# Gathering an expert's rows in quarters and turning them on VectorE instead of TensorE, in a one-core transformer layer on Trainium2

## The chip, the cores and the metric

The kernel runs on one NeuronCore of one Trainium2 chip. A core has five engines with instruction queues of their own, each run in order: TensorE (PE in the rows, PEld for its weight loads), VectorE (DVE), ScalarE (ACT), GpSimd (POOL) and SyncE (SP), and 16 DMA engines that they share. SP issues most of the plain transfers, GpSimd all the indirect ones. The metric is the device time of one execution in microseconds.

## What is computed

The reference is one layer of a diffusion backbone in float32: a token mixer, then a mixture of 64 small experts over 1,024 tokens of width 1,024. The change is in the second half. Each token picks 8 experts, and each expert has two products of 1,024 by 256 (gate and up) and one of 256 by 1,024 (down):

```python
_, idx = lax.top_k(s + b_router, TOP_K)                 # 8 of 64 experts per token
wts = s_sel / jnp.sum(s_sel, axis=-1, keepdims=True) * ROUTE_SCALE
...
xb = hpad[rows]                                          # the rows of one block of one expert
y = (jax.nn.silu(xb @ we_gate[e]) * (xb @ we_up[e])) @ we_down[e]
return acc.at[rows].add(y * rw[:, None].astype(y.dtype)), None
...
shared = (jax.nn.silu(hf @ ws_gate) * (hf @ ws_up)) @ ws_down
return (acc[:nt] + shared).reshape(B, T, D)
```

So 8,192 rows are gathered, sent through their expert's products, weighted and added back; a shared expert runs over all 1,024 tokens besides.

## The kernel before

A first part (mixer and router, about 570 us) writes the normalised rows to DRAM as `hx`, 1,024 rows of 1,024 features followed by the token's 64 expert weights (`XW` = 1,088 columns), and builds on chip, for each of 98 blocks, a column of row numbers: `tok` for the gather, `dst` for the scatter.

Then `moe` runs the experts' stage. `BLOCKS` lists 102 blocks: four of the shared expert (tiles of 128 tokens; three at the head, one at the end) and 98 of the routed experts, 48 of 128 rows, 23 of 80 to 120, 16 of 64 and 11 of 32. The last four token tiles of the shared expert are done in `final`. `pipeline.run` goes through the blocks in software-pipelined order. In the turn of block i it issues gate and up products of block i (`stage_gu`), the down product and the scatter of block i-1 (`stage_dn`), the turning of the hidden vector of block i (`stage_ht`), then `stage_x` of block i+2 and `gather` of block i+3. The order in each engine's queue is made by a scheduler from this program; a gather waits until its buffer, one of three (`xg`), has been read.

- `gather` (L1429 on) is one indirect DMA on GpSimd's queue (L1439): up to 128 rows of 1,088 values, one per partition. Rows beyond the list are skipped by the bounds check.
- `stage_x` (L1444 on) turns the rows, since TensorE wants features on partitions: eight transposes of 128 by 128 through TensorE into PSUM (`px`, L1461; L1454 for blocks of 64 and 32 rows). For the larger blocks the turned rows are then split into a rounded high part and a low remainder: ACT casts (`xH`, L50) and VectorE subtracts (`xL`, L51), each in two halves of 512 columns. Small blocks are copied by ACT only (`xR`).
- `row_weight` (L1347) picks the row's weight out of the 64 gathered with it, one VectorE instruction and an accumulator read.
- The weights of an expert, three parts of 1 MB, are loaded by SP (L1426) into a pool of buffers (`u`) and split in the same way: cast on ACT, subtraction on VectorE (`u<-u,u`, both inputs in SBUF, 128 x 1,024, L50 and L51). Blocks of more than 64 rows use three matmuls per product (L436 to L438, the split parts), smaller blocks one.
- The scatter (L1559) is an indirect DMA on GpSimd that adds the block's result into one of two accumulators (`acc`) in DRAM.

[...]

## Time and profile before

| | us |
|---|---|
| median of three runs (1,494.69 to 1,501.90) | 1,495.82 |
| the profiled execution | 1,497.91 |
| its span in the trace | 1,496.1 |
| TensorE busy in the span | 1,426.1 (95%) |
| VectorE | 1,133.3 (76%) |
| ScalarE | 753.7 (50%) |
| GpSimd | 477.9 (32%) |
| mean load of the 16 DMA engines, 573 to 1,433 us | 0.95 |

The experts' stage lies between the first gather at 573.8 us and the last accumulating write at 1,433 us; what follows is `final`, some 60 us. Busy time is the time in which an engine executes something; an engine that waits in its queue is idle. A row of the timeline gives the start, the length, the engine, the line, the operation, output and inputs, and in brackets the idle time before it and what ended that.

### The profile page before, as it was taken

The page shows a single profiled execution, that of the slowest core. Times are in us where ns is not written, and L with a number is a line of the kernel's source. Part 1 is how long each engine was busy: PE and PEld are TensorE (multiplying, and loading weights), DVE is VectorE, ACT ScalarE, POOL GpSimd, SP SyncE. Part 2 cuts the span into 40 slices and gives each one's busy share as a digit, 9 for nine tenths or more (in the row PEclk, how much of TensorE's full clock was granted, in tenths as well). Part 3 has the DMA queues.
Part 4 walks back from the last instruction along what each step waited for, and adds up shares of the span by engine and source line. Part 5 has one row for each costly group of instructions (what it writes and reads, how often), then busy time and mean ns, then how long its engine had stood idle before and what let it go on. Part 6 is the DMA issues. An engine that isn't in the chain of part 4 may idle for free. (4 is left out here: it accounts for less than half of the span.)

```text
span 1496.1 us, 22962 instructions
## 1 busy us (share of the span) xinstructions
PE 1426.1 (95%) x8211; PEld 1088.5 (73%) x8211; DVE 1133.3 (76%) x1942; ACT 753.7 (50%) x1241; POOL 477.9 (32%) x306
## 2 busy tenths in 40 slices
PE   6999999989999989999999999999999999999975
PEld 4688997765567755876788888888777777777764
DVE  5899979767867886744678788888777877777636
ACT  4421011245433344644566666776676767666621
POOL 1245001112213422233333333333334344455324
PEclk9999999999999999999999999999999999999998
DMA  8421051018653567997999999999999999999975
GB/s 314 176 71 43 1 189 40 19 48 287 221 187 115 193 240 275 357 294 246 306 288 327 331 322 319 333 343 339 316 342 299 321 342 310 315 352 318 337 251 209
DMA packets 94385, 371.64 MB, mean 248 GB/s; under 512 B 18269, under 2 KB 26789, under 8 KB 67770
## 3 DMA queue, kind: packets, MB, share of 16 engines
q1 hardware_dynamic: 65946, 298.48, 53.3%
q0 software_dynamic: 26032, 70.19, 19.2%
q10 hardware_dynamic: 2288, 1.45, 0.4%
q8 instruction: 66, 1.08, 0.3%
q14 instruction: 53, 0.43, 0.1%
HBM read 322.38 MB, written 62.19 MB: 257 GB/s over the span
## 5 line engine op out<-in xcount | busy, mean ns | idle before, releaser
L51 DVE TENSOR_TENSOR u<-u,u 128x1024 fp32r<-128x1024 f32 x354 | 422.0, 1220 | 124.7 <-ACT u L50 94.8
L50 ACT CAST u<-u 128x1024 fp32r<-128x1024 f32 x354 | 361.3, 1052 | 108.5 <-PE pgu L438 41.6
L1559 POOL DMA_INDIRECT acc<-yb,dst x98 | 194.4, 1983 | 351.7 <-ACT hTH L50 118.3
L436 PE MATMUL pgu<-u,xH 128*128 128x512 f32 x608 | 245.8, 404 | 0.4
L437 PE MATMUL pgu<-u,xH 128*128 128x512 f32 x608 | 238.8, 393 | 0.0
L438 PE MATMUL pgu<-u,xL 128*128 128x512 f32 x608 | 238.1, 392 | 0.0
L1439 POOL DMA_INDIRECT xg<-hxd,tok x98 | 123.6, 1261 | 194.1 <-DVE rwj L1347 68.6
L431 DVE SCALAR_TENSOR_TENSOR X<-X,cw 128x912 f32<-128x912 f32 (+14 forms) x120 | 152.0, 1291 | 1.1
L436 PEld LDWEIGHTS pgu<-u,xH 128*128 128x128 f32 x608 | 114.5, 188 | 25.5 <-ACT u L50 2.6
L438 PEld LDWEIGHTS pgu<-u,xL 128*128 128x128 f32 x608 | 114.3, 188 | 24.6
L437 PEld LDWEIGHTS pgu<-u,xH 128*128 128x128 f32 x608 | 114.5, 188 | 21.5
L436 PE MATMUL py<-u,hTH 128*128 128x512 f32 x304 | 122.1, 402 | 0.5 <-ACT hTH L50 0.5
L437 PE MATMUL py<-u,hTH 128*128 128x512 f32 x304 | 119.8, 394 | 0.0
L438 PE MATMUL py<-u,hTL 128*128 128x512 f32 x304 | 118.6, 395 | 0.0
L436 PE MATMUL pf<-hH,wfH 128*128 128x512 f32 x256 | 103.6, 408 | 0.0
L437 PE MATMUL pf<-hL,wfH 128*128 128x512 f32 x256 | 102.7, 401 | 0.7 <-DVE hL L226 0.6
L51 DVE TENSOR_TENSOR xL<-px,xH 128x512 fp32r<-128x512 f32 x152 | 97.5, 681 | 7.7 <-ACT xH L50 7.3
L438 PE MATMUL pf<-hH,wfL 128*128 128x512 f32 x256 | 102.3, 400 | 0.0
L50 ACT CAST xH<-px 128x512 fp32r<-128x512 f32 x152 | 83.9, 592 | 13.7 <-PE pgu L437 7.8
L1551 DVE COPY yb<-py 128x512 f32<-128x512 f32 x75 | 51.5, 687 | 46.3 <-PE py L438 45.8
L51 POOL TENSOR_TENSOR wfL<-wfr,wfH 128x1024 fp32r<-128x1024 f32 x14 | 48.0, 3428 | 118.2 <-ACT wfH L50 104.2
L1461 PE MATMUL px<-ident,xg 128*128 128x128 f32 x600 | 83.8, 274 | 1.1 <-DVE nl L1244 1.1
(431 smaller groups left out, 2515.6 us busy)
## 6 DMA issues: line engine op xcount, KB each, us to landing
u<-in_we_dram SPq DMA_DIRECT2D x192, 1024.0 KB
wa<-in_wa_dram SPq DMA_DIRECT2D x64, 256.0 KB
wa<-in_wa_dram SPq DMA_DIRECT2D x8, 1024.0 KB
wfr<-in_wf_dram SPq DMA_DIRECT2D x16, 512.0 KB
v<-acc SPq DMA_DIRECT2D x16, 512.0 KB
acc<-zero SPq DMA_DIRECT2D x13, 512.0 KB
u<-in_ws_dram SPq DMA_DIRECT2D x6, 1024.0 KB
X<-in_xT_dram SPq DMA_DIRECT2D x8, 512.0 KB
```

The source lines that it names most:

```text
L50: self.nc.scalar.copy(H, src)
L51: return (eng or self.nc.vector).tensor_tensor(L, src, H.bitcast(F32), op=OP.subtract).ins
L431: nc.vector.scalar_tensor_tensor(y[:, :, a:b], u[:, :, a + o:b + o], cw[:, i:i + 1], y[:, :, a:b], op0=OP.mult, op1=OP.add)
L436: mm(out, lH, rH, start=start, stop=False, skip_group_check=free)
L437: mm(out, lH, rL, start=False, stop=False, skip_group_check=free)
L438: mm(out, lL, rH, start=False, stop=stop, skip_group_check=free)
L1439: nc.gpsimd.indirect_dma_start(out=x[:n], out_offset=None, in_=self.hx, in_offset=bass.IndirectOffsetOnAxis(ap=self.tok[:n, c:c + 1], axis=0),
L1461: nc.tensor.transpose(pt[:, k], x[:, (4 * q + k) * 128:(4 * q + k) * 128 + 128], self.ident)
L1551: nc.vector.tensor_copy(y[:, 512:], py)
L1559: nc.gpsimd.indirect_dma_start(out=self.acc[b % NA].rearrange("r (n d) -> (r n) d", n=n), in_=y[:rows], in_offset=None, out_offset=bass.In ...
```

## The change

The gathered rows are no longer turned on TensorE.

- The routed rows come in groups of 32 and quarters of the width. One indirect DMA brings 32 rows: each row of `hx` is read as four rows of 256, and partition 32q + a gets quarter q of row a. A block needs one such DMA per 32 rows, rounded up. Their row numbers are made once, in `route`: the list is bounded from above, copied to the four partition quarters by 16 small matmuls and scaled (`tokq`).
- VectorE then turns all 32 by 32 blocks of the tile in one instruction, from SBUF to SBUF (`STREAM_TRANSPOSE`). Partition 32q + a' of the result holds feature 256q + 32f + a' for f = 0 to 7, and the host lays out the gate and up weights in this order, so that the products run as before.
- The split of the turned rows is one cast and one subtraction of 1,024 columns out of SBUF. Small blocks need no copy. The tile between (`xT`) has one buffer.
- A row's weight is no longer gathered with the row. It is fetched as a single element by an indirect DMA of its own per block (`row_weights`, list `widx`, from the new tensor `hw`) into one of eight columns.
- The shared expert's tiles are loaded by four DMAs each instead of one.

```diff
+        tf = rp.tile([128, NB], F32, name="tf", bufs=1)
+        nc.vector.tensor_scalar(tf, self.tok, 2.0 * NX - 1, None, op0=OP.min)
+        pq = bank("pT4", [128, 4, NB])
+        for g in range(4):
+            for q in range(4):
+                mm(pq[32 * q:32 * q + 32, g], self.ident[:, 32 * g:32 * g + 32], tf, start=True, stop=True,
+                   skip_group_check=True)
+        nc.vector.tensor_scalar(self.tokq, pq, 4.0, self.part[:, 1:2], op0=OP.mult, op1=OP.add)
+        nc.vector.scalar_tensor_tensor(self.widx, tf, float(NE), self.eb, op0=OP.mult, op1=OP.add)
...
-        self.xg = [gp.tile([128, XW], F32, name=f"xg{i}") for i in range(3)]
+        self.xg = [gp.tile([128, 4, 256], F32, name=f"xg{i}") for i in range(3)]
...
-        n = HB if rows == HQ else rows
-        nc.gpsimd.indirect_dma_start(out=x[:n], out_offset=None, in_=self.hx,
-                                     in_offset=bass.IndirectOffsetOnAxis(ap=self.tok[:n, c:c + 1], axis=0),
-                                     bounds_check=NX - 1, oob_is_err=False)
+        for g in range(-(-rows // 32)):
+            nc.gpsimd.indirect_dma_start(out=x[:, g], out_offset=None, in_=self.hx.rearrange("t (q d) -> (t q) d", q=4),
+                                         in_offset=bass.IndirectOffsetOnAxis(ap=self.tokq[:, g, c:c + 1], axis=0),
+                                         bounds_check=4 * NX - 1, oob_is_err=False)
...
+    def load_tile(self, x, j):
+        for q in range(4):
+            self.nc.sync.dma_start(x[32 * q:32 * q + 32], self.hx[128 * j:128 * j + 128, 256 * q:256 * q + 256]
+                                   .rearrange("(g b) d -> b g d", g=4))
+    def row_weights(self, b):
...
+        rw = self.rw[b % 4 + 4 * (rows > HB)]
+        self.nc.gpsimd.indirect_dma_start(out=rw[:n], out_offset=None, in_=self.hw.rearrange("t e -> (t e) ()"),
+                                          in_offset=bass.IndirectOffsetOnAxis(ap=self.widx[:n, c:c + 1], axis=0),
+                                          bounds_check=NX * NE - 1, oob_is_err=False)
...
     def stage_x(self, x, rows=128, native=False):
-            for k in range(8):
-                nc.tensor.transpose(pt[:, k], x[:rows, k * 128:k * 128 + 128], self.ident[:rows, :rows])
-            self.xdone = nc.scalar.copy(R[:, :, :rows], pt).ins
...
-                self.xdone = self.split(H[:, s], L[:, s], pt)
+        n = rows // 32 if native and rows <= HB else 4
+        t = mp.tile([128, 8, 128], F32, name="xR", tag="xH", bufs=2) if native else \
+            mp.tile([128, 8, 128], F32, name="xT", bufs=1)
+        nc.vector.transpose(t[:, :, :32 * n].rearrange("p f (g b) -> p g f b", g=n),
+                            x[:, :n].rearrange("p g (f a) -> p g f a", a=32))
...
+        self.split(H, L, t)
```

**The start of the gathers, GpSimd's queue.** Before, in a row, behind the last step of the lists (`xg` are the three row buffers, `hxd` the rows in DRAM, `tok` the lists):

```order
L1439 DMA xg_5144<-hxd,tok 128x1088
L1439 DMA xg_5145<-hxd,tok 128x1088
L1439 DMA xg_5146<-hxd,tok 128x1088
L1439 DMA xg_5144<-hxd,tok 128x1088
L1439 DMA xg_5145<-hxd,tok 128x1088
L1439 DMA xg_5146<-hxd,tok 128x1088
```

Of the change, at the same place (`rw` are the columns of row weights, `hwd` the weights in DRAM, x4 stands for four in a row):

```order
L1470 DMA rw_136<-hwd,widx 128x1
L1470 DMA rw_133<-hwd,widx 128x1
L1470 DMA rw_134<-hwd,widx 128x1
L1452 DMA xg_5176<-hxd,tokq 128x256 x4
L1452 DMA xg_5177<-hxd,tokq 128x256 x4
L1452 DMA xg_5178<-hxd,tokq 128x256 x4
```

Three weight gathers stand ahead of the first row gather, and each row gather is four.

**The middle of the stage, GpSimd's queue.** Before, one gather and one scatter per block in turn (`acc` are the two accumulators, `yb` the block's result):

```order
L1439 DMA xg_5144<-hxd,tok 96x1088
L1559 DMA acc_63<-yb,dst 1024x1024
L1439 DMA xg_5145<-hxd,tok 88x1088
L1559 DMA acc_64<-yb,dst 1024x1024
L1439 DMA xg_5146<-hxd,tok 96x1088
L1559 DMA acc_63<-yb,dst 1024x1024
```

Of the change:

```order
L1452 DMA xg_5177<-hxd,tokq 128x256 x2
L1581 DMA acc_65<-yb,dst 1024x1024
L1452 DMA xg_5177<-hxd,tokq 128x256 x2
L1452 DMA xg_5178<-hxd,tokq 128x256
L1470 DMA rw_134<-hwd,widx 128x1
L1452 DMA xg_5178<-hxd,tokq 128x256 x3
L1581 DMA acc_64<-yb,dst 1024x1024
```

Between two scatters there are now four row gathers and a weight gather.

**The middle of the stage, VectorE's queue.** Before, one turn of the loop (`u` weight split, `hgu` gate product, `yb` result, `hTL` and `xL` remainders, `rwj` row weight):

```order
L1500 SCALAR_TENSOR_TENSOR hgu<-pgu,rwf,sgu 128x256
L51 TENSOR_TENSOR u_7554<-u_7226,u_7553 128x1024 x2
L1551 COPY yb<-py 128x512
L51 TENSOR_TENSOR hTL<-pht,hTH 128x256
L51 TENSOR_TENSOR xL<-px,xH 128x512 x2
L1347 SCALAR_TENSOR_TENSOR rwj,rwf<-io,eb,xg_5145 128x64
L51 TENSOR_TENSOR u_7657<-u_7251,u_7656 128x1024 x2
```

Of the change:

```order
L1481 STREAM_TRANSPOSE xT<-xg_5178 128x4x8x32
L51 TENSOR_TENSOR u_7589<-u_7196,u_7588 128x1024 x2
L1522 SCALAR_TENSOR_TENSOR hgu<-pgu,rw_136,sgu 128x256
L51 TENSOR_TENSOR xL<-xT,xH 128x1024
L1573 COPY yb<-py 128x512
L51 TENSOR_TENSOR hTL<-pht,hTH 128x256
L51 TENSOR_TENSOR u_7597<-u_7278,u_7596 128x1024
```

The transpose takes its place ahead of the weight split, the remainder of the rows is one instruction with both inputs in SBUF, and the row-weight product is gone.

## Rows read from the trace of the kernel before

**Rows 1.** Page, busy us of each engine over the span.
```profile
PE 1426.1 (95%) x8211; PEld 1088.5 (73%) x8211; DVE 1133.3 (76%) x1942; ACT 753.7 (50%) x1241; POOL 477.9 (32%) x306
```

**Rows 2.** Stretches: us, busy PE, PEld, DVE, ACT, POOL, granted clock, DMA share, GB/s.
```profile
573.00:1433.00 860.00, 856.16 (x4858) 655.65 (x4856) 632.92 (x953) 552.79 (x830) 318.22 (x197) 1.00 0.95 321
900.00:1000.00 100.00, 99.85 (x489) 82.33 (x487) 86.43 (x125) 70.57 (x101) 31.55 (x22) 1.00 0.95 326
...
1200.00:1300.00 100.00, 100.00 (x679) 75.03 (x678) 75.63 (x115) 69.16 (x105) 47.66 (x27) 1.00 0.97 334
1300.00:1400.00 100.00, 100.00 (x723) 73.87 (x722) 77.12 (x120) 69.20 (x109) 52.61 (x27) 1.00 1.00 325
...
1440.00:1496.00 56.00, 38.32 (x168) 30.17 (x168) 31.82 (x45) 13.62 (x28) 23.69 (x15) 0.90 0.64 226
```

**Rows 3.** Waits: who waited for whom, us in total, times, longest.
```profile
SPq L1426 <- DVE u L51: 495.3, 87, 22.5
...
POOL xg L1439 <- DMA acc<-yb,dst: 3.7, 3, 3.0
```

**Rows 4.** The stage's instructions that write or read `px`: PE, PEld, DVE, ACT.
```profile
573.00:1433.00 860.00, 100.17 (x804) 82.95 (x804) 93.64 (x147) 94.73 (x174) 1.00 0.95 321
```

**Rows 5.** Groups by line: count, busy us, mean ns, idle time before.
```profile
L51 DVE TENSOR_TENSOR u<-u,u 128x1024 fp32r<-128x1024 f32 x354 | 422.0, 1220 | 124.7 <-ACT u L50 94.8
...
L51 DVE TENSOR_TENSOR xL<-px,xH 128x512 fp32r<-128x512 f32 x152 | 97.5, 681 | 7.7 <-ACT xH L50 7.3
...
L1347 DVE SCALAR_TENSOR_TENSOR rwj<-io,eb,xg 128x64 f32<-128x64 f32 (+1 forms) x98 | 26.9, 274 | 5.4 <-DMA xg<-hxd,tok 4.8 <-DVE hgu L1500 0.2
L1347 DVE DVE_READ_ACCUMULATOR rwj<-io,eb,xg 128x1 f32 (+1 forms) x98 | 7.8, 79 | 0.0
```

**Rows 6.** Timeline of POOL, late in the stage: gathers of 64, 128 and 64 rows.
```profile
1331.11 2.04 POOL L1439 DMA_INDIRECT xg<-hxd,tok  x1 [1.06 <-DVE rwj L1347]
1334.20 1.05 POOL L1439 DMA_INDIRECT xg<-hxd,tok  x1 [1.05 <-DVE yb L1551]
...
1344.99 0.99 POOL L1439 DMA_INDIRECT xg<-hxd,tok  x1 [1.06 <-DVE rwj L1347]
```

**Rows 7.** Timeline of POOL at the stage's start: first and third gather in a row.
```profile
573.80 1.18 POOL L1439 DMA_INDIRECT xg<-hxd,tok  x1 [7.58 <-DVE tok L1224]
...
577.48 2.03 POOL L1439 DMA_INDIRECT xg<-hxd,tok  x1 [0.30 <-issue]
```

**Rows 8.** Timeline of DVE beside Rows 6 and 7, the weight split.
```profile
575.08 4.70 DVE L51 TENSOR_TENSOR u<-u,u 128x1024 fp32r<-128x1024 f32 x4
...
1331.06 2.54 DVE L51 TENSOR_TENSOR u<-u,u 128x1024 fp32r<-128x1024 f32 x2 [0.41 <-ACT u L50]
...
1334.30 2.35 DVE L51 TENSOR_TENSOR u<-u,u 128x1024 fp32r<-128x1024 f32 x2
...
1344.95 2.53 DVE L51 TENSOR_TENSOR u<-u,u 128x1024 fp32r<-128x1024 f32 x2 [0.42 <-ACT u L50]
```

**Rows 9.** Gathers, scatters and line 51: groups by line, and line 51 in the stage.
```profile
L1439 POOL DMA_INDIRECT xg<-hxd,tok x98 | 123.6, 1261 | 194.1 <-DVE rwj L1347 68.6
L1559 POOL DMA_INDIRECT acc<-yb,dst x98 | 194.4, 1983 | 351.7 <-ACT hTH L50 118.3
...
573.00:1433.00 860.00, 539.31 (x573) 0.00 (x0) 1.00 0.95 321
```

**Rows 10.** Timeline of PE: the eight transposes of one block.
```profile
909.16 1.04 PE L1461 MATMUL px<-ident,xg 128*128 128x128 f32 x8
```

**Rows 11.** Timeline of POOL at the end of the stage.
```profile
1386.47 2.04 POOL L1439 DMA_INDIRECT xg<-hxd,tok  x1 [1.07 <-issue]
...
1428.37 1.56 POOL L1559 DMA_INDIRECT acc<-yb,dst  x1 [6.42 <-ACT hTH L50]
1432.71 0.96 POOL L1557 DMA_DIRECT2D acc<-yb  x1 [2.79 <-ACT xH L50]
```

**Rows 12.** DMA queues over the span: packets, MB, share of 16 engines.
```profile
q10 hardware_dynamic: 2288, 1.45, 0.4%
```

More of the change, by code (lines that the diff above doesn't have):

```diff
@@ L892, in run @@
         dp, dp_ = self.pool("dram", 1, DRAM)
-        self.hx = dp.tile([NX, XW], F32, name="hxd")
+        self.hx = dp.tile([NX, D], F32, name="hxd")
+        self.hw = dp.tile([NX, NE], F32, name="hwd")
         self.x1d = dp.tile([NX, D], F32, name="x1d")
@@ L954, in route_consts @@
         self.eb = T("eb", [128, NB])
-        self.rw = [T(f"rw{i}", [128, 1]) for i in range(4)]
+        self.rw = [T(f"rw{i}", [128, 1]) for i in range(8)]
         for t in self.rw:
@@ L965, in mixer_out @@
         self.pair = fp.tile([128, 64], F32, name="pair")
+        self.tokq = fp.tile([128, 4, NB], I32, name="tokq")
+        self.widx = fp.tile([128, NB], I32, name="widx")
         rk, self.rk_ = self.pool("rk", 1)
@@ L1299, in spill @@
             T = lambda n, s, d=F32: tp.tile(s, d, name=n)
-            x = T("oxg", [128, XW])
+            x, xp, xw = T("oxg", [128, D]), T("oxp", [128, 8, 128]), T("oxw", [128, NE])
             nc.vector.memset(x, 0.0)
+            nc.vector.memset(xw, 0.0)
             with tc.For_i(0, nl, 1) as i:
@@ L1311, in spill @@
                                              bounds_check=NX - 1, oob_is_err=False)
+                nc.gpsimd.indirect_dma_start(out=xw, out_offset=None, in_=self.hw,
+                                             in_offset=bass.IndirectOffsetOnAxis(ap=ti[:, 0:1], axis=0),
+                                             bounds_check=NX - 1, oob_is_err=False)
                 rw = T("orw", [128, 1])
-                self.row_weight(T("oej", [128, NE]), x, ei, rw)
-                xT = T("oxT", [128, 8, 128])
+                nc.vector.scalar_tensor_tensor(T("oej", [128, NE]), self.io[:, :NE], ei, xw, op0=OP.is_equal,
+                                               op1=OP.mult, accum_out=rw)
+                nc.vector.tensor_copy(xp.rearrange("p f (q a) -> p f q a", q=4),
+                                      x.rearrange("p (q f a) -> p f q a", q=4, f=8))
+                xT = x.rearrange("p (k r) -> p k r", k=8)
                 for q in range(2):
@@ L1342, in spill @@
             self.close(op_)
-    def row_weight(self, junk, x, e, out):
-        n = out.shape[0]
-        self.nc.vector.scalar_tensor_tensor(junk[:n], self.io[:n, :NE], e[:n], x[:n, D:], op0=OP.is_equal, op1=OP.mult,
-                                            accum_out=out)
     def compact(self, rp, sl, width, outs, eq):
@@ L1457, in stage_x @@
-        for q in range(2):
-            s = slice(4 * q, 4 * q + 4)
-            pt = self.bank("px", 4, 128)
-            for k in range(4):
-                nc.tensor.transpose(pt[:, k], x[:, (4 * q + k) * 128:(4 * q + k) * 128 + 128], self.ident)
-            if native:
-                nc.scalar.copy(R[:, s], pt)
-            else:
-                self.xdone = self.split(H[:, s], L[:, s], pt)
-        return (R,) if native else (H, L)
+        n = rows // 32 if native and rows <= HB else 4
@@ L1468, in mm6 @@
+        return H, L
     def mm6(self, out, x, w, k, nk, s):
@@ L1644, in stage_x @@
             def stage_x(i):
-                v, (_, _, rows, c) = g.pop(i), BLOCKS[i]
-                out = self.stage_x(v, rows, raw[i])
-                rw[i] = None
-                if c is not None:
-                    rw[i] = self.rw[i % 4] if rows <= HB else mp.tile([128, 1], F32, name="rwf", bufs=4)
-                    with self.tc.issue_after(self.xdone):
-                        self.row_weight(mp.tile([128, NE], F32, name="rwj", bufs=1), v, self.eb[:, c:c + 1],
-                                        rw[i][:HB] if rows <= HB else rw[i])
-                return out
+                rw[i] = self.row_weights(i)
+                return self.stage_x(g.pop(i), BLOCKS[i][2], raw[i])
             for i in range(i0, i0 + 2):
@@ L1689, in pipeline @@
         for j in range(SE, 8):
-            nc.sync.dma_start(row(("h", j)), self.hx[128 * j:128 * j + 128, :D])
-        self.x = {j: self.stage_x(self.rows["h", j]) for j in range(SE, min(SE + 2, 8))}
+            self.load_tile(row(("h", j)).rearrange("p (g d) -> p g d", g=4), j)
+        self.x = {j: self.stage_x(self.rows["h", j].rearrange("p (g d) -> p g d", g=4)) for j in range(SE, min(SE + 2, 8))}
         for j in range(8):
@@ L1709, in gu @@
             if j + 2 < 8:
-                self.x[j + 2] = self.stage_x(self.rows["h", j + 2])
+                self.x[j + 2] = self.stage_x(self.rows["h", j + 2].rearrange("p (g d) -> p g d", g=4))
             return self.stage_gu(self.x[j], self.shared)
```

29 lines of the change are left out of this document (15 added, 14 removed).

## The prediction

> **What bounds the kernel now.** I read the busy shares first [rows 1], then the experts' stage by itself [rows 2], then who waits for whom [rows 3], then single rows of the timeline. The stage runs from the first gather, 573.8 [rows 7], to the end of the last accumulating write, 1,433.7 [rows 11]. [...] VectorE is at 632.9 us (74%), and in its fullest 100 us at 86.4. GpSimd (POOL) is at 318.2 us and the 16 DMA engines at a share of 0.95 [rows 2]. The weights are not late: their queue on SP waits 495 us for buffers that VectorE's weight split frees [rows 3]. [...]
>
> **What the change takes from TensorE.** All turning of gathered rows: 804 transposes in the stage, 100.2 us of TensorE by the row of that tile alone [rows 4]. [...] The copies out of PSUM go too: per tile of 128 rows two subtractions of 681 ns become one of 1,220 ns on a 1,024-wide SBUF tile, the price of the weight split [rows 5]. ACT loses the same halves and the copies of the small blocks; it was busy for 553 of 860 us [rows 2], so I price that at nothing, and it can't cost, since one cast replaces two.
>
> **VectorE.** Added: one transpose per block. No row of before shows one. Lower bound: half a 1,024-wide row, 0.6 us; upper: two of them, 2.4 us; I take one, 1.22 us, the nearest row (same width, SBUF to SBUF, four-byte elements) [rows 5]. 75 tiles x 1.22 = 92 us, and for 16 blocks of 64 and 11 of 32 rows, by width, 14. The subtraction is 75 x (1.22 - 1.36) = -10. The row-weight product and its read-back go: 98 x (0.274 + 0.079) = -35 [rows 5]. Sum 633 + 61 = 694 us, 81% of the stage, which fits; with a transpose of 2.4 us it is some 800, or 93%, which does not fit under the 86% that VectorE reached in its fullest stretch.
>
> [...]
>
> **GpSimd.** Here the work grows. Before, a block had one gather and one scatter on this queue. Now it has one gather per 32 rows (57 blocks of 104 to 128 rows have 4, 14 of 80 to 96 have 3, 16 of 64 have 2, 11 of 32 have 1: 313 in all), one gather of row weights (98) and the scatter (98).
>
> What does one cost? A gather's length hardly goes by its rows: one of 64 rows at 1,344.99 lasts 0.99 us, one of 128 at 1,334.20 lasts 1.05 [rows 6], and 0.93 to 1.05 is the floor of all 98 (I use 1.03). So a quarter-gather costs as much as a whole one; the work is per instruction. Two in a row stand 0.30 us apart: the third at the stage's start had waited for nothing but its issue [rows 7]. On top comes a stall: one that starts inside a VectorE subtraction of two SBUF tensors (the weight split) lasts to the end of that instruction plus the floor. At 1,331.11 it starts 0.05 us into one at 1,331.06 and lasts 2.04; at 1,334.20 it starts before one at 1,334.30 and lasts 1.05 [rows 6, 8]. The third of three in a row, under a run of such subtractions, lasted 2.03 [rows 7, 8]. The mean over all 98, stalls included, is 1.261 us, so 0.23 is stall; the scatter's mean is 1.983 [rows 9].
>
> Sum of the queue: (313 + 98) x (1.26 + 0.30) = 641 us, 98 x (1.98 + 0.30) = 223 us, together **864 us**, against an 860 us stage. Bounds of the stall: at nothing, 411 x 1.33 + 98 x 1.87 = 730 us (a scatter's floor is 1.56 to 1.58 [rows 11]). At random starts: subtractions of two SBUF tensors, 1.22 us each, would fill 58% of the stage (539 us of that line [rows 9], less 97 with a PSUM input [rows 5] and some 32 of the hidden vector, which has one too, plus 75 x 1.22: about 500), so 0.58 x 0.61 = 0.36 us, and the queue is 411 x 1.69 + 223 = 918 us. I take the mean that the trace has, since a stalled instruction restarts at the end of a subtraction and the next one then tends to miss it.
>
> **Where it starts and ends.** The lists reach the gathers later: a minimum (0.24 us, as the other small operations there), 16 small matmuls (two groups of 8 at the 1.04 us of a group of 8 transposes [rows 10]), one 392-wide scaling out of PSUM (about 0.5): 3 us, so 576.8. The three weight gathers that stand ahead of the first row gathers are in the sum. At the end, before, the last gather was issued at 1,386.5 and the last scatter at 1,428.4 [rows 11], 42 us, because gathers ran ahead of TensorE. If GpSimd is late they do not; then the last block's landing, turning, both products and the shared tile remain, which I put at 25 us (two blocks of some 9 us and 7 for landing and turning), with four scatters inside (9 us). End: 576.8 + 864 - 9 + 25 = 1,457, against 1,433.7: **+23 us**. Nothing is queued behind the waits that costs more: in GpSimd's order gathers of a later block and the scatter of an earlier one alternate, and the scatter's input is long there when the queue is late.
>
> **Edits at nothing.** SP gets 12 more issues for the shared tiles and a separate write of the weights; its queue already waits for buffers 495 us [rows 3], and 12 issues at some 0.4 us are 5 us if that cover were gone. The spill loop doesn't run. The weight layout is host work and moves no byte. The last four tiles trade 32 transposes for 4 on VectorE under a chain of GpSimd and DMA: 0, at most the four transposes, +5, at least -2, half the 32 transposes' 4.2 us.
>
> **Transfers.** Gathered bytes stay (8,192 rows; 64 columns fewer), but a row is four packets. Lower bound: nothing. Upper: each extra packet at 42 ns, the mean packet of q10, the queue of small packets (0.4% of 16 engines over 1,496 us, by 2,288) [rows 12]: 24,600 x 42 ns / 16 = 65 us on 817. I take 20, a share of 0.95 again in a stage of 883 us.
>
> **Rivals.**
> (a) GpSimd keeps up, and part of TensorE's 100 us arrives: faster. The point that decides is the mean stall of the 411: the stage breaks even with a queue of 841 us, a stall of 0.17 us. At 0.10 (and scatters stalled by 0.2) the queue is 588 + 203 = 791 us, the stage ends at 1,384, -50 us: 1,446. VectorE allows that (694 of 810, its fullest share so far) and hardly more. For it: starts can fall favourably, as at 1,344.99, 0.04 us into a subtraction [rows 8] and not stalled. Against: VectorE gets 92 us more of the instructions that stall, and gathers come in bursts.
> (b) The same queue within 0.15 to 0.19 us of stall: no change.
> (c) VectorE: transposes at 2.4 us, 800 us at 0.9 is 889: +29, 1,525.
> (d) Transfers: the four-packet rows cost the upper 65 us: 882 us of DMA time at the 0.98 of the fullest 200 us [rows 2] is 900: +40, 1,536; gathers land late and transposes hold VectorE's queue. So far only 3.7 us of GpSimd's waits are for landings [rows 3].
> [...]
> That the transposes stay on TensorE is excluded by the instruction order.
>
> **How the numbers follow.** The forecast (GpSimd's queue becomes the bound) has 0.50, (a) 0.29, (b) 0.12, (c) 0.04, (d) 0.05. The profiled execution took 1,497.9 (span 1,496.1), 2.1 above the median of 1,495.8; with +23 on the median I predict **1,519 us**. The forecast's own range is 1,503 to 1,573 (stall up to 0.36: queue 918, +77). The range that should hold 8 in 10 reaches to (a): 1,450 to 1,573. About 0.5% is what a measurement of this kernel can tell from no change; faster by more 0.29, within 0.12, slower 0.59.
>
> **What would show it.** Right: GpSimd above 70% busy in the stage with gaps of 0.30 between its DMAs and hardly a wait, row gathers of 1.2 to 1.4 us mean, TensorE down to some 755 us busy with holes ahead of the gate product, VectorE waiting for gathers. Wrong: quarter-gathers well under 1 us, or stalls under 0.17 (then (a)); a transpose row of 2 us or more (c); GpSimd waiting for DMA (d). [...]

## The result, and the profile after

The changed kernel takes **1,564.45 us** (median of 4 runs, 1,554.78 to 1,568.13) where the kernel before takes 1,498.05: a ratio, by rounds, of 1.0432, 95% interval 1.0376 to 1.0489. The prediction was 1,519, in a range of 1,450 to 1,573: it is slower, and in part for the reason named, but the loss is 66 us, not 23. The profiled execution took 1,568.13 (span 1,566.2), 70.2 more than that of before.

Where they went is read from three kinds of rows on GpSimd: the first row of its indirect DMAs in the stage, the end of the last row gather, the end of the last accumulating write. First, the start of the gathers and the end of the stage in the timeline of GpSimd, after (start, length, engine, line, operation, output and input, and in brackets the idle time ahead and what ended it); they answer to [rows 7] and [rows 11]:

```profile
576.05 1.20 POOL L1470 DMA_INDIRECT rw<-hwd,widx  x1 [7.06 <-DMA u<-in_we_dram]
...
580.18 1.96 POOL L1452 DMA_INDIRECT xg<-hxd,tokq  x1 [0.30 <-DVE u L51]
582.45 1.00 POOL L1452 DMA_INDIRECT xg<-hxd,tokq  x1 [0.30 <-issue]
583.75 1.00 POOL L1452 DMA_INDIRECT xg<-hxd,tokq  x1 [0.30 <-issue]
585.05 1.00 POOL L1452 DMA_INDIRECT xg<-hxd,tokq  x1 [0.30 <-issue]
...
1434.52 1.36 POOL L1452 DMA_INDIRECT xg<-hxd,tokq  x1 [0.31 <-issue]
1436.19 1.02 POOL L1452 DMA_INDIRECT xg<-hxd,tokq  x1 [0.31 <-issue]
1437.51 1.64 POOL L1581 DMA_INDIRECT acc<-yb,dst  x1 [0.30 <-ACT sgT L1533]
1439.45 1.38 POOL L1470 DMA_INDIRECT rw<-hwd,widx  x1 [0.30 <-ACT u L50]
1444.83 2.15 POOL L1581 DMA_INDIRECT acc<-yb,dst  x1 [4.00 <-DMA acc<-yb,dst]
1448.03 1.87 POOL L1581 DMA_INDIRECT acc<-yb,dst  x1 [1.05 <-issue]
1457.38 1.57 POOL L1581 DMA_INDIRECT acc<-yb,dst  x1 [7.48 <-DMA acc<-yb,dst]
1462.88 1.57 POOL L1581 DMA_INDIRECT acc<-yb,dst  x1 [3.92 <-DVE yb L1573]
1469.25 1.95 POOL L1581 DMA_INDIRECT acc<-yb,dst  x1 [4.80 <-ACT sgT L1533]
1477.88 1.57 POOL L1581 DMA_INDIRECT acc<-yb,dst  x1 [6.68 <-ACT hTH L50]
1482.21 0.98 POOL L1579 DMA_DIRECT2D acc<-yb  x1 [2.75 <-DVE yb L1573]
```

So the time splits as follows. "Predicted" is the working of the prediction put on the same marks.

| stretch, us | before | predicted | after | difference |
|---|---|---|---|---|
| first indirect DMA of the stage at | 573.8 | 576.8 | 576.05 | +2.3 |
| to the end of the last row gather | 814.7 | 855 | 861.2 | +46.5 |
| to the end of the last accumulating write | 45.2 | 25 | 46.0 | +0.8 |
| to the end of the span | 62.4 | 62.4 | 83.0 | +20.6 |

The predicted differences were +3, +40, -20 and 0. The gather stretch is nearly as reckoned; the next two lines hold the error, some 21 us each.

The groups of GpSimd's instructions in the stage, after (count, busy time and mean length in ns, idle time ahead and what ended it), against [rows 9]:

```profile
L1452 POOL DMA_INDIRECT xg<-hxd,tokq x313 | 390.6, 1248 | 115.6 <-issue 73.7 <-DVE xT L1481 20.1 <-DVE u L51 8.9
L1581 POOL DMA_INDIRECT acc<-yb,dst x98 | 181.8, 1856 | 61.9 <-issue 18.8 <-DMA acc<-yb,dst 11.8 <-ACT hTH L50 9.9
L1470 POOL DMA_INDIRECT rw<-hwd,widx x98 | 123.9, 1264 | 36.6 <-issue 16.8 <-DMA u<-in_we_dram 7.4 <-DVE u L51 5.2
```

Gathers of a quarter and of single elements last 1,248 and 1,264 ns in the mean, the 1.26 us of the forecast; 509 instructions are 696 us, with 0.30 ahead of each 849. The next rows are the stretches before and after the last row gather, the last phase, and the last 59 us before the last row gather by themselves (busy time of each engine, granted clock of TensorE, load of the DMA engines), against [rows 2]:

```profile
576.00:1437.00 861.00, 774.97 (x3885) 569.36 (x3874) 670.77 (x746) 511.48 (x700) 682.37 (x501) 0.95 0.90 301
1437.00:1483.00 46.00, 39.66 (x210) 26.25 (x208) 28.29 (x33) 21.41 (x33) 14.70 (x10) 0.96 1.02 294
1483.00:1566.00 83.00, 39.21 (x152) 30.73 (x152) 36.89 (x46) 14.12 (x26) 21.84 (x16) 0.74 0.51 180
1378.00:1437.00 59.00, 59.00 (x397) 41.61 (x396) 49.96 (x58) 39.76 (x58) 47.23 (x36) 0.96 0.94 306
```

In the 861 us GpSimd executes 501 instructions for 682 us, with their gaps 833: all other waits come to no more than some 28. TensorE, which set the pace before (busy for 856.2 of the 860 us at a granted clock of 1.00 [rows 2]), has holes: 775 of 861 us busy. Its granted clock is 0.95 there. VectorE is at 671 us. Neither of them is full over the stretch, but TensorE is in its last 59 us: the holes lie before. The waits, against [rows 3] (who waits at which line, for what, total, times, longest):

```profile
POOL xg L1452 <- issue: 73.7, 241, 0.5
ACT yb L1571 <- DMA acc<-yb,dst: 67.6, 17, 10.8
...
DVE xT L1481 <- DMA xg<-hxd,tokq: 59.8, 10, 13.1
...
PE pht L1538 <- DVE hgu L1522: 51.1, 16, 9.4
```

Those for landings (scatters that hold result buffers, 67.6 us; gathered rows, 59.8) are the rival reading of these rows: that the stage waits for transfers, not for GpSimd's instructions.

### The profile page after: what moved, and what is told of

It is laid out like the page before. It is cut to its first block, busy times and chain, and to the rows that moved or that the text cites. A ratio compares the mean times of both kernels' runs of the same rounds, so it can differ in the third digit from the quotient of the medians.

```text
span 1566.2 us, 21840 instructions
## 1 busy us (share of the span) xinstructions
PE 1378.2 (88%) x7389; PEld 1023.8 (65%) x7395; DVE 1205.8 (77%) x1783; ACT 727.3 (46%) x1130; POOL 847.9 (54%) x619
## 3 DMA queue, kind: packets, MB, share of 16 engines
q0 software_dynamic: 32176, 67.78, 18.4%
## 5 line engine op out<-in xcount | busy, mean ns | idle before, releaser
L1452 POOL DMA_INDIRECT xg<-hxd,tokq x313 | 390.6, 1248 | 115.6 <-issue 73.7
L436 PE MATMUL pgu<-u,xH 128*128 128x512 f32 x608 | 249.2, 411 | 6.8 <-DVEq L1264 6.5
L437 PE MATMUL pgu<-u,xH 128*128 128x512 f32 x608 | 244.0, 401 | 1.2 <-DVE u L51 1.2
L1581 POOL DMA_INDIRECT acc<-yb,dst x98 | 181.8, 1856 | 61.9 <-issue 18.8
L436 PE MATMUL py<-u,hTH 128*128 128x512 f32 x304 | 127.1, 418 | 36.1 <-DVE v L1742 23.7
L1481 DVE STREAM_TRANSPOSE xT<-xg 128x1024 f32<-128x1024 f32 x72 | 89.1, 1237 | 79.2 <-DMA xg<-hxd,tokq 59.8
L1470 POOL DMA_INDIRECT rw<-hwd,widx x98 | 123.9, 1264 | 36.6 <-issue 16.8
L436 PEld LDWEIGHTS pgu<-u,xH 128*128 128x128 f32 x608 | 118.0, 195 | 34.1 <-issue 9.2
L437 PEld LDWEIGHTS pgu<-u,xH 128*128 128x128 f32 x608 | 118.0, 194 | 27.3 <-DVE u L51 3.9
L437 PE MATMUL py<-u,hTH 128*128 128x512 f32 x304 | 122.2, 402 | 0.0
L51 DVE TENSOR_TENSOR xL<-xT,xH 128x1024 fp32r<-128x1024 f32 x76 | 92.6, 1218 | 35.4 <-ACT xH L50 29.3
L50 ACT CAST xH<-xT 128x1024 fp32r<-128x1024 f32 x76 | 79.7, 1048 | 69.9 <-DVE xT L1481 34.3
L51 POOL TENSOR_TENSOR wfL<-wfr,wfH 128x1024 fp32r<-128x1024 f32 x14 | 40.9, 2918 | 124.6 <-ACT wfH L50 110.6
```

Source lines behind the costliest of these rows:

```text
L50: self.nc.scalar.copy(H, src)
L51: return (eng or self.nc.vector).tensor_tensor(L, src, H.bitcast(F32), op=OP.subtract).ins
L436: mm(out, lH, rH, start=start, stop=False, skip_group_check=free)
L437: mm(out, lH, rL, start=False, stop=False, skip_group_check=free)
L1452: nc.gpsimd.indirect_dma_start(out=x[:, g], out_offset=None, in_=self.hx.rearrange("t (q d) -> (t q) d", q=4), in_offset=bass.IndirectOffs ...
L1470: self.nc.gpsimd.indirect_dma_start(out=rw[:n], out_offset=None, in_=self.hw.rearrange("t e -> (t e) ()"), in_offset=bass.IndirectOffsetOn ...
```

## Experiments

Three readings of the loss are tested: GpSimd's queue sets the stage (Q), landings set it (L), and the order in the final phase costs its part (T). Each line below is the profiled execution cut at the same three marks, and the median against the kernel before on the same chip. The cuts are of one execution, which lies up to 12 us from the median (in after_final_order 12 below it, in after_final_order_2 12 above).

| kernel | GpSimd DMAs | first to last gather | to last write | to end | median | ratio to before (95%) |
|---|---|---|---|---|---|---|
| changed kernel | 510 | 861 | 46 | 83 | 1,564.5 | 1.0432 (1.0376, 1.0489) |
| after_dummy | 608 | 993 | 43 | 83 | 1,693.8 | 1.1282 (1.1248, 1.1315) |
| after_no_weights | 412 | 791 | 46 | 81 | 1,487.5 | 0.9898 (0.9862, 0.9934) |
| after_one_quarter | 295 | 750 | 49 | 83 | 1,459.4 | 0.9714 (0.9683, 0.9745) |
| after_more_results | 510 | 866 | 45 | 82 | 1,570.9 | 1.0491 (1.0436, 1.0545) |
| before_single_weights | 295 | 814 | 47 | 63 | 1,498.6 | 1.0002 (0.9979, 1.0024) |
| before_pieces | 426 | 822 | 45 | 62 | 1,508.6 | 1.0061 (1.0032, 1.0089) |
| before_full_queue | 524 | 857 | 43 | 63 | 1,540.0 | 1.0288 (1.0240, 1.0336) |
| after_final_order | 510 | 857 | 45 | 76 | 1,562.3 | 1.0433 (1.0381, 1.0485) |
| after_final_order_2 | 510 | 872 | 46 | 66 | 1,547.7 | 1.0312 (1.0286, 1.0338) |
| after_no_weights_order | 412 | 795 | 46 | 64 | 1,472.2 | 0.9834 (0.9792, 0.9876) |
| weights_in_quarters | 412 | 900 | 55 | 67 | 1,593.2 | 1.0628 (1.0608, 1.0648) |
| weights_in_quarters_2 | 412 | 893 | 48 | 67 | 1,588.5 | 1.0631 (1.0590, 1.0672) |
| packets_1152 | 412 | 781 | 45 | 63 | 1,468.8 | 0.9810 (0.9785, 0.9835) |
| weights_in_quarters_3 | 412 | 823 | 46 | 68 | 1,509.4 | 1.0085 (1.0053, 1.0117) |
| weights_on_vector | 412 | 830 | 42 | 66 | 1,511.9 | 1.0091 (1.0074, 1.0108) |
| weights_on_vector_a | 412 | 811 | 47 | 68 | 1,505.2 | 1.0044 (1.0028, 1.0061) |
| weights_in_quarters_a | 412 | 822 | 51 | 67 | 1,517.5 | 1.0119 (1.0103, 1.0135) |
| four_row_buffers | 412 | 781 | 56 | 67 | 1,484.6 | 0.9911 (0.9895, 0.9928) |

### Does GpSimd's queue set the stage?

**after_dummy**: more instructions and hardly a byte.

```diff
+        self.nc.gpsimd.indirect_dma_start(out=self.mp.tile([32, 1], F32, name="dm", bufs=8), out_offset=None,
+                                          in_=self.hw.rearrange("t e -> (t e) ()"),
+                                          in_offset=bass.IndirectOffsetOnAxis(ap=self.widx[:32, c:c + 1], axis=0),
```

> The changed kernel with one more gather per block on GpSimd: 32 single elements of the row weights into a small tile that nobody reads (98 instructions, hardly any bytes). Theory Q (GpSimd's queue of DMA instructions sets the experts' stage): every one of them costs its 1.03 to 1.26 us and the 0.30 us ahead of it, so the time grows by 98 x 1.33 to 98 x 1.56, 130 to 153 us: 1,695 to 1,717. Theory L (the stage waits for landings: scatters that hold the result buffers, 67.6 us of ACT's waits, and gathered rows, 59.8 us of VectorE's): landings hardly change, under 20 us: below 1,585. Theory C (TensorE's clock in the holes): under 20 us too.

1,693.8, 129 us more. The new group, in the trace of this kernel:

```profile
L1473 POOL DMA_INDIRECT dm<-hwd,widx x98 | 94.6, 966 | 29.9 <-issue 29.6 <-DMA u<-in_we_dram 0.3
```

98 x (0.966 + 0.30) is 124 us, and the gather stretch grew by 132. The time follows the count of instructions; the bytes stayed (369.1 and 369.2 MB). Theory L, and TensorE's clock as the cause (C), allowed 20 us at most. The queue pays 1.27 us for each, 0.966 and the 0.30 ahead of it.

**after_no_weights**: less of the same; every row weight is 1, so the weighting of the rows is left out.

```diff
-        self.nc.gpsimd.indirect_dma_start(out=rw[:n], out_offset=None, in_=self.hw.rearrange("t e -> (t e) ()"),
...
+        return self.rw[b % 4 + 4 * (rows > HB)]
```

> The changed kernel without the 98 gathers of row weights: every row weight is 1, so the weighting of the rows is left out. Theory Q: GpSimd's queue of 849 us loses 98 x (1.264 + 0.30) = 153 and is at 696; it no longer sets the stage. [...] Theory L: scatters and gathered rows land as late as before, so at most 15 us: 1,550 or more.

1,487.5: 77 us less, where L had 15 at most, and 11 below the kernel before. For Q my estimate was 25 to 60 us less (1,505 to 1,540), from the load of the DMA engines in the changed kernel's trace (0.90 of 864 us and 1.00 of the next 63). So the queue is the limit, and the DMA engines let the stage shrink further than I had put it.

**after_one_quarter**: `for g in range(1)` in `gather`; all rows of a block but the first 32 are left out.

> The changed kernel with only the first of the quarter-gathers of every block (98 instead of 313); the other rows of a block stay zero, so those rows' part of the result is left out. All the rest is done as before. Theory Q: GpSimd's queue falls to 849 - 215 x 1.55 = 516 us and the DMA engines lose the packets too, so the stage falls to TensorE's 756 us plus holes or VectorE's 673: some 780 us, end at about 1,440 to 1,470. If the DMA engines are what stands next behind the queue, this is 50 us or more below the kernel without weight gathers; if TensorE or VectorE is, the two are within 20 us. Theory L: the gathered rows land early, the scatters as late as before: a gain of 20 to 40 us, 1,525 to 1,545.

1,459.4, as Q has it, 28 below the kernel without weight gathers. First to last gather is 750 us, and there TensorE is busy for 735.8 of them at a granted clock of 1.00: TensorE is the limit again. The 28 us fall between the two expectations (50 or more, 20 or less), and this kernel also moves fewer bytes, so it stays open whether TensorE or the DMA engines stand next behind the queue.

**after_more_results**: `name="yb", bufs=4` in place of 3 (and smaller tiles in the spill loop, which doesn't run).

> The changed kernel with four result buffers (yb) instead of three, so that ScalarE's copy of a block's result waits for an older scatter (67.6 us in the changed kernel's trace). Theory L (those landings cost the stage): 20 to 40 us less, 1,525 to 1,545. Theory Q (GpSimd's queue sets the stage; what waits for the scatter waits for the queue): 0 to 6 us less, 1,558 to 1,565.

1,570.9, no gain. With it the scatters' part of theory L falls too; after_dummy had spoken against both parts.

**before_single_weights, before_pieces, before_full_queue**: the other way round, the change's instructions in the kernel before, transposes on TensorE. The first has `row_weights` alone, the second the cut gathers alone, the third both.

```diff
+        k = 4 if rows > HB else rows // 32
+        t, w = {4: self.tok4, 2: self.tok2, 1: self.tok.unsqueeze(1)}[k], XW // k
+        for q in range(k):
+            nc.gpsimd.indirect_dma_start(out=x[:n, w * q:w * q + w], out_offset=None,
+                                         in_=self.hx.rearrange("t (q d) -> (t q) d", q=k),
+                                         in_offset=bass.IndirectOffsetOnAxis(ap=t[:n, q, c:c + 1], axis=0),
```

> The kernel before with one part of the change alone: row weights as 98 single-element gathers, in place of VectorE's product over 64 gathered columns and its read-back. GpSimd's queue 376 + 153 = 529 of 860 us, VectorE 35 us less. Theory Q: the queue is not full and TensorE sets the stage: within 6 us of the kernel before, 1,493 to 1,506. Rival (single-element gathers land late and hold VectorE's hidden vectors): 1,515 or more.

> The kernel before with the gather alone in pieces: four column quarters of 272 elements for blocks of over 64 rows, two halves for 64, one for 32; 327 gathers instead of 98, rows in four packets, all transposes still on TensorE and the row weights still in the gathered columns. GpSimd's queue: 98 x 1.56 + 98 x 2.28 = 376 us and 229 x 1.56 = 357 more, 733 of the stage's 860: not full. Theory Q: within 6 us of the kernel before, 1,494 to 1,506. Rival D (rows in four packets: the transfers come late, or the DMA engines' 817 us grow past the stage): 20 to 50 us more, 1,518 to 1,550.

> The kernel before with as many instructions on GpSimd's queue as the changed kernel has: its gathers in pieces as in before_pieces (327) and the row weights as 98 single-element gathers. All transposes stay on TensorE. Queue: 425 x 1.56 + 98 x 2.28 = 886 us against 860 of TensorE's work, which were 376 in the kernel before and 733 in before_pieces. Theory Q, with the two ends as the changed kernel has shown them: last gather at 580 + 886 - 18 for the last eight scatters = 1,448, 46 us from there to the last accumulating write, 62 for the final phase in its old order: some 1,555 (1,540 to 1,575). Rival: the queue only sets the time in company with the transposes on VectorE or the new weight layout: 1,505 to 1,520, as before_pieces.

1,498.6: nothing, as expected. 1,508.6: 10 us, between the two expectations; 4 of them are the later start (578.0; six more steps on the lists), the rest the stage, in which TensorE is busy for 814 of 822 us. 1,540.0: 43 us, at the lower edge of Q's range but far above the rival. Its instructions are 395.9 + 173.5 + 115.4 us and 523 gaps of 0.30, 842 in all; in the gather stretch of 857 us it executes 516 for 673 us, with their gaps 828, and TensorE, with all its transposes, is busy for 828 too. So against the 197 of the kernel before 295 cost nothing, 426 some 10 us and 524 some 43: little or nothing while the queue is shorter than TensorE's work, dear from there.

### The end of the kernel

In the changed kernel and in those above that change its stage alone the final phase takes 81 to 83 us, in the kernel before 62. VectorE's timeline tells why. The first addition of `final` in the kernel before, and the first small step of the norm behind it:

```profile
1445.80 1.22 DVE L1729 TENSOR_TENSOR v<-v,v 128x1024 f32<-128x1024 f32 x1 [10.72 <-DMA v<-acc]
1448.24 0.15 DVE L1146 TENSOR_SCALAR ssf<-ssf 128x1 f32<-128x1 f32 x1 [1.22 <-ACT sq L1143]
```

The same in the changed kernel, with the hidden vectors of the shared expert's tiles (`hgu`) ahead of it:

```profile
1497.51 0.42 DVE L1520 TENSOR_TENSOR hgu<-pgu,sgu 128x256 f32<-128x256 f32 x1
...
1501.64 0.43 DVE L1520 TENSOR_TENSOR hgu<-pgu,sgu 128x256 f32<-128x256 f32 x1 [1.02 <-ACT sgu L1517]
...
1510.05 0.42 DVE L1520 TENSOR_TENSOR hgu<-pgu,sgu 128x256 f32<-128x256 f32 x1 [5.12 <-ACT sgu L1517]
...
1515.77 0.42 DVE L1520 TENSOR_TENSOR hgu<-pgu,sgu 128x256 f32<-128x256 f32 x1 [3.88 <-ACT sgu L1517]
1516.11 1.22 DVE L1744 TENSOR_TENSOR v<-v,v 128x1024 f32<-128x1024 f32 x1
1518.55 0.15 DVE L1148 TENSOR_SCALAR ssf<-ssf 128x1 f32<-128x1 f32 x1 [1.22 <-ACT sq L1145]
```

In the kernel before the first addition (`v<-v,v`) ran 12 us after the last accumulating write, when its loads had come. In the changed kernel the hidden vectors of all four shared tiles stand ahead of it, three of them waiting for ScalarE, and it runs 33 us after the write.

**after_final_order, after_final_order_2**: the gate products of tiles 5 to 7 are queued behind the first addition on VectorE, and in the second kernel (whose edit follows) behind the last step and the squares of output tiles 0 to 2 on VectorE and ScalarE.

```diff
-                    h = gu(j + 1)
+                    with tc.issue_after(self.ends[j - 4][0]), tc.issue_after(self.ends[j - 4][1]):
+                        h = gu(j + 1)
```

> The changed kernel with the order of the last phase held: the gate products of the shared expert's tiles 5 to 7 stand behind the first addition of the final sums on each engine's queue. In the changed kernel VectorE's queue has the hidden vectors of all four shared tiles ahead of that addition, which starts at 1,516 although the loads it needs were issued at 1,487. Theory T (the order of that queue makes the end late): the first addition starts some 16 us earlier and the end follows: about 1,548. Rival: the shared tiles' products are needed anyway and only change places with the additions: 0 to 4 us, 1,560 to 1,565.

> As after_final_order, with ScalarE's queue held as well: the gate products of the shared expert's tiles 5 to 7 stand behind the squares of output tiles 0 to 2 there, and behind these tiles' last instruction on VectorE. In after_final_order the first addition did start 17 us after the last accumulating write instead of 33, but VectorE's next step then waited 8.7 us for ScalarE's squares, which stood behind the same products. Theory T (the order of the queues makes the end late): now the 12 to 20 us arrive: 1,545 to 1,553. Rival (the products of the shared tiles and the loads of the sums are what the end waits for, in whichever order): within 4 us of the changed kernel, 1,560 to 1,568.

The first missed: 1,562.3, as its rival had it. VectorE's rows show where the gain stayed; the addition ran at 1,489.06, 16 us after the last accumulating write, and then its queue waited for ScalarE's squares:

```profile
1489.06 1.22 DVE L1745 TENSOR_TENSOR v<-v,v 128x1024 f32<-128x1024 f32 x1
...
1500.45 0.15 DVE L1148 TENSOR_SCALAR ssf<-ssf 128x1 f32<-128x1 f32 x1 [8.71 <-ACT sq L1145]
```

With both queues held the phase takes 66 us and the median is 1,547.7, 17 less.

**after_no_weights_order**: no weight gathers (the weighting left out) and the final order held.

> The changed kernel without the gathers of row weights (all weights 1, so the weighting is left out) and with the final order of after_final_order_2. If queue and final order are separate causes, their gains add: 1,487 - 17 = 1,470 (1,464 to 1,477). If the final order pays only where the stage is late, it stays at 1,483 to 1,490.

1,472.2: the two costs add. The two tests also meet from the other side: the changed kernel with the final order held is at 1.0312 of the kernel before, and before_full_queue, with as many DMAs and all its transposes on TensorE, at 1.0288, with intervals that overlap. So queue and final order explain the loss, and little of it is left for the transposes on VectorE and the weight layout.

### What stands right behind the queue

Seven versions, and one test between them, try to have the gain for good: the row weights travel in the gathered rows again (no gathers of their own), and the final order is held.

**weights_in_quarters, _2, _3**: 32 columns of weights behind every quarter; a small transpose on VectorE (`xw`) and a one-column product on TensorE pick the weight (the edit is that of the second).

```diff
+        xw = self.mp.tile([64, 4, 32], F32, name="xw", bufs=4)
+        self.nc.vector.transpose(xw[:, :n], x[:64, :n, 256:])
...
+            mm(ps[r:r + k], xw, self.ohe[:, c:c + 1], start=True, stop=True, skip_group_check=True)
```

> A version for speed: the changed kernel with the row weights back in the gathered rows (32 columns behind every quarter, 288 elements to a packet), so the 98 single-element gathers go; 32x32 transposes of these columns on VectorE and one product with a one-hot column per block on TensorE give the weights. The final order is held as in after_final_order_2. Theory Q: GpSimd's queue loses 98 x 1.56 = 153 us as in after_no_weights (1,487), the final order gives 10 to 20, and the longer packets and small transposes take some 5 to 10: 1,470 to 1,490, below the kernel before (1,500). Rival: VectorE (704 of 857 us in after_no_weights, and 98 x 0.2 = 20 more) or the DMA engines (0.96 of the stage) are full: 1,495 or more.

> weights_in_quarters mended: there VectorE's small transpose of the weight columns stood between other work and held the gathers' buffers (GpSimd waited 61.7 us for it, it waited 121 us for landings), and ScalarE's copy of the weights held that queue. Now the small transpose is VectorE's first step on a gathered tile, the one-column product stands right ahead of the block's gate product, and VectorE reads the weights from PSUM. If these places were the cause: 1,470 to 1,490, below the kernel before. If a gathered tile with two readers on VectorE is late wherever they stand, or the packets of 1,152 bytes are: 1,540 or more, as in weights_in_quarters (1,593).

1,593.2 and 1,588.5, some 90 us slower than the kernel before, although the 98 instructions (153 us with their gaps in the changed kernel) are gone from GpSimd's queue. VectorE's largest wait in the second, and with it GpSimd's for the buffers:

```profile
DVE xw L1469 <- DMA xg<-hxd,tokq: 120.8, 26, 10.7
POOL xg L1451 <- DVE xT L1494: 81.9, 29, 12.2
```

The small transpose stands in VectorE's queue ahead of work that is ready, and waits there for a gather; the second kernel, made to mend that, kept it there. packets_1152 gathers the same rows and leaves the weights unused; in _3 the small transpose is queued behind the large one.

> after_no_weights_order (1,472) with the rows of weights_in_quarters: quarters of 288 elements are gathered, 1,152 bytes to a packet, but the 32 columns of weights are used by nobody (all weights 1, the weighting is left out). It has the queue and the transposes of after_no_weights_order. If the longer packets are what made weights_in_quarters late: 1,550 or more. If the place of the small transposes is: 1,470 to 1,485 (the bytes of the gathers are 12% more, some 0.03 of the DMA engines' time in the stage at most).

> weights_in_quarters_2 with the small transpose held behind the large one of the same block on VectorE's queue, so that it never is the first to wait for a landing (120.8 us of such waits in weights_in_quarters_2). If that head of VectorE's queue was the cause: the queue of GpSimd is then 696 us as in after_no_weights_order and the time 1,472 plus 5 to 20 for the small steps: 1,477 to 1,492, below the kernel before (1,497). If not: 1,550 or more.

1,468.8, for 1,472.2 in after_no_weights_order: the longer pieces (1,152 bytes for 1,024) cost nothing. 1,509.4: 79 us came back by the order of two instructions, and VectorE's largest wait for gathers is 29.0 us in all there, in place of the 120.8. A step that stands first in the queue while a gather has not landed holds all of VectorE.

**weights_on_vector, weights_on_vector_a, weights_in_quarters_a**: 40 us are left. All 64 weights behind every quarter, and one masked product on VectorE instead of TensorE's; then, in the "a" kernels, the second half of each result copied by ScalarE.

```diff
+        self.nc.vector.scalar_tensor_tensor(self.mp.tile([128, 4, NE], BF, name="rwj", bufs=1)[:p, :n], i,
+                                            self.eb[:p, c:c + 1], x[:p, :n, 256:], op0=OP.is_equal, op1=OP.mult,
+                                            accum_out=rw[:p])
```

> A version for speed, and a test of what the 40 us between packets_1152 (1,469) and weights_in_quarters_3 (1,509) are. There one-column products gave TensorE 33 us more (218 rows of 234 ns) where it is busy for 801 of 847 us. Here all 64 weights lie behind every quarter (320 elements, 1,280 bytes to a packet), and one masked product with a running sum on VectorE, right behind the block's transpose, picks the weight on its own partition: 71 x 0.5 + 27 x 0.35 = 45 us for VectorE (705 of 847), nothing for TensorE. If TensorE is the limit that stands next behind the queue: 1,469 plus 5 to 15, 1,474 to 1,484, faster than the kernel before (1,498). If VectorE's queue is: 1,500 or more.

> weights_on_vector with the second half of every result tile copied out of PSUM by ScalarE (busy for 519 of 847 us there) instead of VectorE: 75 copies of 682 ns, 51 us, leave VectorE (715 of 847), 75 x 0.59 = 44 go to ScalarE. If VectorE, at 96 to 98% in the stage's fullest 300 us, is the limit that the 43 us of weight products ran into: back by 25 to 43 us, 1,470 to 1,487, faster than the kernel before (1,498). If the 40 us come from elsewhere (landings, the DMA engines, which are at 1.00 there): 1,500 to 1,520.

> weights_in_quarters_3 with the same copies moved to ScalarE. There the weights cost TensorE 33 us and VectorE some 24. If VectorE is the limit: 1,470 to 1,490; if TensorE is: 1,500 or more, whatever happens to VectorE.

1,511.9, 1,505.2 and 1,517.5: neither TensorE's load nor VectorE's is it by itself. What was left to try is GpSimd's wait for the last reader of a row buffer, in weights_on_vector_a:

```profile
POOL xg L1451 <- DVE rwj L1469: 69.7, 26, 9.4
```

**four_row_buffers**: one buffer more (the space is that of the last norm's gain, loaded later).

```diff
-        self.xg = [gp.tile([128, 4, 320], F32, name=f"xg{i}") for i in range(3)]
+        self.xg = [gp.tile([128, 4, 320], F32, name=f"xg{i}") for i in range(4)]
```

> weights_on_vector_a with four row buffers (xg) instead of three; the space comes from the gain vector of the last norm, which is now loaded into one of them for the final phase. In weights_on_vector_a GpSimd waited 69.7 us, 26 times, for VectorE's weight product, the last reader of the buffer that the next gather fills, and VectorE waited 52.4 us for landings: a ring of gather, landing, transpose, weight product over three buffers. If that ring is what costs the versions with weights in the rows their 40 us, a fourth buffer takes 25 to 45 us off: 1,460 to 1,480, faster than the kernel before (1,498). If the waits only move (to VectorE's own load, TensorE or the DMA engines): 1,495 or more.

1,484.6, 21 us less: short of the 25 to 45, but the wait shrank:

```profile
POOL xg L1448 <- DVE rwj L1466: 41.1, 18, 6.1
```

This version leaves nothing of the work out and is 0.9% faster than the kernel before: 0.9911 (0.9895 to 0.9928). The fourth buffer gives the 21 us, but the size of that wait doesn't order the kernels: it is 36.2 us in packets_1152 (1,468.8) and 35.6 in weights_on_vector (1,511.9). So what the 40 us are is shown in part only, and where the 16 us above packets_1152, which does no weighting, lie was not settled.

## Why the prediction was wrong in size

**Right.** GpSimd's queue became the bound, through the number of its instructions: adding 98 costs 129 us, taking 98 away gives 77, and the kernel before, its transposes left on TensorE, becomes 43 us slower by as many DMAs. The prices held: gathers 1.25 us for 1.26, single elements 1.26 for 1.26, scatters 1.86 for 1.98, gaps of 0.30, a queue of 849 for 864; the first instruction 2.3 us later for 3. The transpose took 1,237 ns for a full tile where 1,220 was forecast:

```profile
L1481 DVE STREAM_TRANSPOSE xT<-xg 128x1024 f32<-128x1024 f32 x72 | 89.1, 1237 | 79.2 <-DMA xg<-hxd,tokq 59.8 <-issue 19.3
```

VectorE's sum of 694 us came out at 699 (670.8 + 28.3 in the two windows). TensorE lost its transposes, but in the stage it is busy for 815 us (775 + 39.7) and not 755, at a granted clock of 0.95 to 0.96; that added nothing to the gather stretch, which is about as long in before_full_queue (857 us for 861) at a granted clock of 0.99. That the time lies inside the stated range is luck: its slow end was made for stalls of 0.36 us, and they are 0.22 (1.25 less the 1.03). The reason given for the lower figure, that the gather after a stalled one tends to miss the next subtraction, is not what the timeline shows: of 75 row gathers issued some 0.3 us after a stalled one 32 last over 1.15 us themselves, of 124 after one that was not stalled 35.

**Wrong: the end of the stage.** "If GpSimd is late they do not [run ahead]; then the last block's landing, turning, both products and the shared tile remain, which I put at 25 us." They do run ahead. Behind the last row gather six scatters and the plain write were still to come before, and seven after, and from there to the last accumulating write it takes 46.0 us, as the 45.2 before, and 42 to 56 in all nineteen kernels here. The -20 us should have been 0. What failed is the condition: GpSimd was not late at the end. The last 59 us before the last row gather have 19 row gathers beside 9 scatters (313 beside 98 in all; towards the end blocks of 128 and of 32 rows alternate). GpSimd's queue is full there too (47.2 us and 36 gaps of 0.30), but TensorE is busy for 59.00 of the 59 (the row above), so it had nothing to wait for; in the other kernels it is busy for 54 to 59 of the same stretch. What the end would be with GpSimd late to the last gather is in none of these runs. [rows 11] had shown the stretch; the reason given for it was not in the rows.

**Wrong: the final phase.** "The last four tiles trade 32 transposes for 4 on VectorE under a chain of GpSimd and DMA: 0, at most [...] +5." The transposes are not what costs; the order on VectorE's and ScalarE's queues is, which the scheduler made anew (why it put the shared tiles first is not shown). +20.6 us in the trace, 17 of it given back by holding the order. This was to be read in the instruction order before the run.

With 0 and +21 in these two places and the queue as it was, the sum is +23 + 20 + 21 = +64, and 6 more in the gather stretch make the 70: the queue there was 833 us long and not 855, but had some 28 us of waits that the sum left out. That the stretch came out so near is in part luck: these two errors nearly cancel.

**The rivals.** (a), GpSimd keeping up, had the price 1,446. Even with 153 us less on the queue and the old order held at the end it is 1,472: the prediction gave (a) a stage of 810 us, into which the DMA engines' 817 us of transfers [rows 2] don't go; in packets_1152 their load is 0.98 over the whole gather stretch:

```profile
574.00:1356.00 782.00, 742.74 (x3836) 553.65 (x3836) 667.67 (x743) 510.26 (x700) 583.85 (x405) 0.98 0.98 337
```

(c), slow transposes, and (d), late transfers, are excluded by the 1,237 ns and by after_more_results, packets_1152 and before_pieces (10 us at most for rows in pieces). (d) also counted 24,600 more packets; the profile has 6,144 more in q0, the queue of these DMAs (32,176 for 26,032), and 3,136 of them go with the weight gathers (29,040 in after_no_weights). Gathering in pieces costs time here through the instructions on GpSimd's queue and, as far as packets_1152 and before_pieces show, not through the bytes per piece.

## What to carry to other kernels

Cost an indirect DMA by the instruction, not by its rows: some 1.0 us and a gap of 0.3 on GpSimd here, and in the changed kernel over 1.15 us for 118 of the 144 row gathers that start while VectorE subtracts two SBUF tensors; a queue of 197 that is busy for 37% of the stage took 295 for nothing, and from the length of the bounding engine's work on each one costs its full price (129 us for 98). When work changes engine, read the new order of every in-order queue, above all at the end, and which instruction stands first in one while a transfer has not landed. Ask of the last blocks by themselves which engine is late there: the bound of the whole stage need not be that of its end.

## What the runs showed of the hardware that I had not expected

A gather of 32 single elements holds GpSimd for 966 ns, about as long as one of 128 pieces of 1 KB (the rows at 582.45 to 585.05 above: 1.00 us).

The stalls stayed at some 0.2 us in the mean (1,248 ns against a floor of 1.0) although the change made the row subtractions read both inputs from SBUF. Which gathers are stalled is sharp in the changed kernel's trace: of its 313 row gathers 144 start while VectorE subtracts two SBUF tensors (weights or rows), and 118 of these last over 1.15 us; 169 start while VectorE is idle, transposes, or reads PSUM, and none of these does. Why such a subtraction holds them is not shown.

How much of such work VectorE has doesn't settle the mean, though. With 40 us of products over two SBUF tensors added (weights_on_vector) the 313 gathers go from 1,316 ns in the mean to 1,411, some 30 us of queue; in weights_on_vector_a and four_row_buffers, with the same products, they are at 1,330 and 1,323. Why was not settled. The group of gathers in packets_1152, then in weights_on_vector, weights_on_vector_a and four_row_buffers:

```profile
L1451 POOL DMA_INDIRECT xg<-hxd,tokq x313 | 411.8, 1316 | 143.4 <-issue 74.4 <-DVE xT L1475 36.2 <-DVE tokq L1235 9.2
...
L1451 POOL DMA_INDIRECT xg<-hxd,tokq x313 | 441.7, 1411 | 142.3 <-issue 66.2 <-DVE rwj L1469 35.6 <-DVE xT L1480 11.0
...
L1451 POOL DMA_INDIRECT xg<-hxd,tokq x313 | 416.4, 1330 | 170.3 <-issue 76.8 <-DVE rwj L1469 69.7 <-DMA u<-in_we_dram 8.4
...
L1448 POOL DMA_INDIRECT xg<-hxd,tokq x313 | 414.0, 1323 | 143.2 <-issue 76.9 <-DVE rwj L1466 41.1 <-DVE tokq L1230 9.2
```
